# Four places in the output block products of a hybrid encoder layer: a first read, a deviation, a low part and an offset in PSUM

## The chip, the cores and the metric

One core of one Trainium2 chip runs the whole layer in one launch. The metric is the device time of one launch in microseconds (us); the median of several runs is compared. The engines are named as in the profile: PE (TensorE matmuls; PEld its weight loads), DVE (VectorE), ACT (ScalarE), POOL (GpSimd) and SP (SyncE, whose queue issues the DMAs here).

## What is computed

The layer projects 2048 tokens of width 1024, runs a gated linear attention (group A) and a latent softmax attention (group B), gates both, joins them to a 2048 x 1024 matrix and multiplies it by one 1024 x 1024 output matrix. Then comes the residual with a layer norm. The change touches only this last part:

```python
def layer_norm(t, g, b):
    mu = jnp.mean(t32, axis=-1, keepdims=True)
    var = jnp.mean(jnp.square(t32 - mu), axis=-1, keepdims=True)
    y = (t32 - mu) * lax.rsqrt(var + LN_EPS) * g + b
...
    o_b = mla_branch(...)        # ends with  o * jax.nn.silu(gate)
    mixed = jnp.concatenate([o_a, o_b], axis=-1) @ w_out
    x = layer_norm(DEEPNORM_ALPHA * x + mixed, ln_g[layer], ln_b[layer])
```

## The kernel before

The kernel goes through the sequence in 16 chunks of 128 tokens. Every product in fp32 is made of three matmuls: both operands are split into a high part (`hi`, a copy on ACT to the format fp32r, L400) and a low part (`lo`, operand minus high part, here on POOL, L406), and `mm3` (L454 to L456) adds high x high, high x low and low x high in PSUM.

**Chunks 0 to 7** of the output projection are plain: two halves n of 512 columns, eight k-steps each (`OutProj.part`). For each chunk the operand is loaded (`load`), split (`split` calls `op.hi` and `op.lo` for the two halves j = 0, 1; the second half is first multiplied by the gates on POOL, `op.gate`, L2271), multiplied, added to ALPHA * x on DVE (`residual`, L2320) and normalised: `finish_a` on DVE (statistics, then (row - mean) * ln_g, L2336), `rsqrt` on ACT in six small steps (L2342 to L2347), `finish_b` on DVE (row * scale + ln_b, L2353) and the store.

`op.ln` holds the two vectors ln_g and ln_b, first as copies in SBUF (`ln_sb`, the tiles lng and lnb); `ln_psum(0)` and `ln_psum(1)` copy them on ACT (L2220) into two PSUM tiles, and what is traced after that reads them there.

**Chunks 8 to 15** are done in four pairs (class `Pair`, p = 0 to 3). A pair takes two chunks (r = 0 is the odd one, r = 1 the even one) and the two halves of their columns as 2 x 2 blocks A11, A12, A21, A22 and forms the four output blocks with seven products instead of eight (Winograd's form of Strassen's scheme). DVE makes four sums S1 to S4 of the blocks (`add`, L2030): S1 = A21 + A22, S2 = S1 - A11, S3 = A11 - A21, S4 = A12 - S2; each operand is split into high and low part (A11h, A11l and so on). The gates of A12 and A22 are two multiplications on POOL each (`gate`, L2018). The products are P1 (A11), P5 (S1), P6 (S2), P3 (S4), P7 (S3), P2 (A12) and P4 (A22), in this order in pairs 0 to 2; the last pair has P2 ahead of P7, and P4 in two halves. They go to four PSUM banks: P1 and P7 to bank 0, P5 and P2 to bank 1, P6 to bank 2, P3 and P4 to bank 3 (in the last pair P2 to bank 0 and P7 to bank 1).

Each product is read on DVE into the output blocks: `read` (R1 for P1, R5 and R5b for P5, R2, R3, R4b for sums in bank 2, R6 for P3, R7 for P2, R4 for P4). The first read of a block is row = ALPHA * x + bank (L2065), further ones add (L2067). So R1 reads bank 0 and needs the x rows, which `load_res` fetches. `c1` and `c7` (`copy`, L2055, tile pc) copy bank 0 to SBUF on ACT, and `U2`, `U3` (`sum`, L2058) add that copy to bank 2 on DVE.

A finished pair is normalised while the next one runs. Row 1: statistics and `finish_a`, `rsqrt`, `finish_b`, as above. Row 0: `squares` on ACT (sum and sum of squares, L2083 to L2087, called sq in the table of places), `scale` on ACT (called rs: L2092, L2093 and then the six steps of `rsqrt`), `centre` on DVE (L2098), then `finish_b`. In pair 2 the last step is `finish_off` on ACT and POOL instead.

**What sets the order.** Every step of this part is put on one list with a place in us (`put`), counted from the start T of its pair; pairs are 19.05 us apart. The list is sorted, traced in that order, and `in_order` ties each instruction to the one before it on its engine. So a place is not a time: it only says what goes ahead of what on each engine, and an instruction that waits holds all behind it on its engine. Accesses of two engines to one PSUM tile are put in the order in which they are traced, reads too. The places of pairs are in `PLACE_PAIR`: `add`, `hi`, `lo`, `gate` and `gate0` to `gate2` for the loads and splits; `read` for pairs 0 to 2, `read_last` for pair 3; `first` and `second` override some of `add`, `hi` and `lo` for pairs 0 and 1:

```python
second=dict(lS4=-0.85),
first=dict(hA11=-15.2, hS3=-8.0, hA12=0.9, lS3=-6.5, aS4=0.3, hS4=0.35, lS4=0.4),
```

A pair's places below zero stand among those of the pair before: the gates of pair 3 (`gate`, -19.94 to -21.3 and so on) are at -5.67, -2.25, -0.89 and 0.47 of pair 2. Chunks 4 and 5 and the splits of 6 and 7 are written out by hand (`fixed`), with the order kept on ACT, POOL and SP only.

Of the kernel before, what the change touches and what calls it, by code (L numbers as in the profile page):

```python
# [84 lines left out]
    lo=(11.99, 11.22, 11.21, 12.62, 11.98, 11.51, 10.87, 10.63),  # L85
# [23 lines left out]
    lo=(15.35, 16.07, 20.38, 20.41, 24.45, 25.82, 33.5, 36.25),  # L109
# [24 lines left out]
PAIR0, PAIR_US = 8, 19.05  # L134
# [5 lines left out]
    gate=((-19.94, -18.58), (-24.72, -21.3)),  # L140
    add=dict(S1=-10.55, S3=-9.85, S2=-7.6, S4=-0.95),
    hi=dict(A11=-17.26, S1=-9.75, S2=-7.0, A12=-2.0, S3=-4.77, S4=-0.9, A22=-2.66),
    lo=dict(A11=-13.14, S1=-8.45, S2=-6.5, S3=-3.67, A22=1.77, A12=3.13, S4=4.49),
    product=dict(P1=0.0, P5=2.72, P6=5.44, P3=8.16, P7=10.88, P2=13.6, P4=16.32),
    last=dict(P1=0.0, P5=2.72, P6=5.44, P3=8.16, P2=10.88, P7=13.6, P4=16.32),
    gate2=((-11.9, -10.6), (-18.0, -16.7)),
# [1 line left out]
    gate0=((-6.0, -4.7), (-24.72, -21.3)),  # L148
    second=dict(lS4=-0.85),
    first=dict(hA11=-15.2, hS3=-8.0, hA12=0.9, lS3=-6.5, aS4=0.3, hS4=0.35, lS4=0.4),  # L150
    read=dict(c1=2.78, R1=5.9, R5=6.5, R5b=7.1, U2=9.9, R2=10.5, R6=11.3, c7=14.91, U3=15.63, R3=16.26, bn22=16.89,
              R7=17.52, sq=18.25, R4=20.34, R4b=20.97, bn21=21.6, rs=21.9, fa=(22.9, 22.23), fb=(23.9, 26.7), late=(24.2, 24.8)),
    lnb=-1.5,
    read_last=dict(c1=2.78, R1=3.3, R5=6.3, R5b=6.9, U2=8.9, R2=9.5, R3=10.1, R4b=10.7, R6=11.5, bn12=12.1,
                   R7=14.1, bn11=14.7, R3p=16.9, R4p=17.5, bn22=18.1, fa=(15.3, 20.2), fb=(17.0, 20.3)),
)
# [62 lines left out]
    lo=(-0.5, 0.357),  # L219
# [79 lines left out]
    lo=(-0.452, -1.813),  # L299
# [65 lines left out]
    lo=(-0.124, 0.045),  # L365
# [24 lines left out]
class K:  # L390
# [1215 lines left out]
    def attention(self):  # L1606
# [4 lines left out]
        with ExitStack() as ctx:  # L1611
# [214 lines left out]
            op = OutProj(self, ctx, qp, bp, sp, pS, pM, pX, pO, pA)  # L1826
# [5 lines left out]
            def put(place, fn, *a):  # L1832
                todo.append((place, len(todo), fn, a))
# [23 lines left out]
            for k in range(NK):  # L1857
                if k < PRE_W:
                    v = NP * (PRE_BLOCK + k)
                    hi, lo = v + out["pre_hi"], v + out["pre_lo"]  # L1860
                else:
                    hi = end + out["w_hi"] + (k - PRE_W) * out["w_step"]
                    lo = hi + out["w_lo"]
# [30 lines left out]
            late = dict(last)  # L1894
# [8 lines left out]
            def split(c):  # L1903
                if c < NCH:
                    op.hi(rest[c], 0)
                    op.lo(rest[c], 0)
                    op.gate(rest[c])
                    op.hi(rest[c], 1)
                    op.lo(rest[c], 1)

            pairs = [Pair(op, p, PAIR0 + 2 * p + 1, PAIR0 + 2 * p) for p in range((NCH - PAIR0) // 2)]
            with fixed():
                load(4)
                for c in (2, 3):
                    op.load_res(rest[c])
                load(5)
                split(4)
                load(6)
                op.load_res(rest[4])
                for c in (0, 1):  # L1920
                    op.finish(rest[c])
                split(5)
                load(7)
                op.load_res(rest[5])
                op.fetch_t("2l")
                op.fetch_t("3h")
                for c in (2, 3):
                    op.residual(rest[c], 0)
                    op.residual(rest[c], 1)
                    op.finish(rest[c])  # L1930
            for c in (4, 5):
                with fixed():
                    if c == 4:
                        split(6)
                        pairs[0].load(1)
                        op.product(rest[4])
                    else:
                        op.load_res(rest[6])
                        tsum(nb - 1)
                        with self.after(rest[4]["last"]):  # L1940
                            rcp(nb - 1)
                        op.product(rest[5])
                        op.ln_psum(0)
                        pairs[1].load(0, "of")
                        op.fetch_t("3m")
                        split(7)
                        pairs[0].load(0)
                    op.finish(rest[c])
                if c == 4:
                    with self.after(*last.values()), fixed():  # L1950
                        for f in (tot, oh, ol):
                            f(nb - 1)
# [13 lines left out]
                put(t + 2 * half + (5 if c == 6 else 4), op.finish_b, o)  # L1966
            for place, f in ((5.4, turn), (5.41, y), (6.5, rows), (6.51, yc)):
                put(place, f, nb - 1)
            put(3.5, op.ln_psum, 1)
            put(17.15, op.fetch_t, "4h")  # L1970
            put(17.16, op.fetch_t, "4l")
            op.last_pair = pairs[-1]
# [7 lines left out]
class Pair:  # L1980
# [131 lines left out]
    def put(self, put, T, last):  # L2112
# [24 lines left out]
        if last:  # L2137
            reads = (("R1", 0, 0, 0), ("R5", 1, 1, 1), ("R5b", 0, 1, 1), ("R2", 0, 1, 2), ("R3", 1, 1, 2), ("R4b", 1, 0, 2),
                     ("R6", 0, 1, 3), ("R7", 0, 0, b["P2"]), ("R3p", 1, 1, b["P7"]), ("R4p", 1, 0, b["P7"]))
        else:  # L2140
            at(e["c7"], self.copy, bank[b["P7"]])
            at(e["U3"], self.sum, bank[2])
            reads = (("R1", 0, 0, 0), ("R5", 1, 1, 1), ("R5b", 0, 1, 1), ("R2", 0, 1, 2), ("R6", 0, 1, 3), ("R3", 1, 1, 2),
                     ("R7", 0, 0, b["P2"]), ("R4", 1, 0, 3), ("R4b", 1, 0, 2))
        for n, r, h, x in reads:
# [277 lines left out]
```

## Time and profile before

| | us |
|---|---|
| median of 3 runs (lowest, highest) | 1287.73 (1287.08, 1287.99) |
| the profiled execution, its own time | 1284.93 |
| its span, first to last instruction | 1283.2 |
| PE busy | 1255.9 (98%) |
| DVE busy | 940.3 (73%) |
| ACT busy | 875.0 (68%) |
| POOL busy | 851.2 (66%) |

The mean granted clock of PE is 0.998. In a list in order of time a row has the start in us, the busy time in us, the engine, the line, the operation, out<-in with the tiles' names, the shape, the count of instructions that are merged into the row, and in brackets the idle time ahead of it with what ended it. Successive instructions of one engine overlap a little, so a row's start can lie before the end of the row ahead. A row of waits has the total, the number of times and the longest.

In this profile pair 0's P1 starts at 1195.03 us, pair 1's at 1214.07, pair 2's at 1234.53 and pair 3's at 1256.13; the last matmul starts at 1275.21.

### The profile page before, as it was taken

How to read it: one execution, taken by the hardware profiler on the slowest of the kernel's cores; microseconds unless marked ns; L12 is line 12 of the kernel's file. 1: busy time of each engine (PE TensorE's matmuls, PEld its weight loads, DVE VectorE, ACT ScalarE, POOL GpSimd, SP SyncE). 2: the span in 40 equal slices, each digit the busy share in tenths (PEclk: the TensorE clock that was granted, in tenths of full speed). 3: DMA queues.
4: the chain of work that ended last, by engine and by line, in shares of the span. 5: the costliest groups of instructions: out<-in, count | busy, mean ns of one | idle time of the engine just before them, and what ended most of it. 6: DMA issues, size and time to landing. Idle time of an engine off the chain costs nothing.

```text
span 1283.2 us, 20179 instructions
## 1 busy us (share of the span) xinstructions
PE 1255.9 (98%) x6928; PEld 1109.2 (86%) x6928; DVE 940.3 (73%) x1702; ACT 875.0 (68%) x1553; POOL 851.2 (66%) x550
## 2 busy tenths in 40 slices
PE   7999999999999999999999999999999999999997
PEld 7999999999989999999788888888888888788876
DVE  6866674656675445555798888888888888648887
ACT  6765657666675665665688888888888888613455
POOL 0244545363657666672188888889999999955774
PEclk9999999999999999999999999999999999999999
DMA  9332525343575565555501111121223211468952
GB/s 297 94 97 63 168 79 161 99 151 104 185 249 164 178 226 189 181 194 169 172 1 41 42 42 41 42 58 58 58 58 91 58 49 37 169 211 310 333 186 93
DMA packets 122518, 166.81 MB, mean 130 GB/s; under 512 B 18502, under 2 KB 71118, under 8 KB 121776
## 3 DMA queue, kind: packets, MB, share of 16 engines
q1 hardware_dynamic: 114256, 163.39, 40.0%
q0 software_dynamic: 768, 2.10, 0.5%
q8 instruction: 55, 0.90, 0.3%
q10 hardware_dynamic: 7392, 0.03, 0.3%
q14 instruction: 47, 0.39, 0.2%
HBM read 106.72 MB, written 58.75 MB: 129 GB/s over the span
## 4 chain that ended last, share of the span: by engine, by line
PE 56%; POOL 3%; issue 3%; DVE 3%; DMA 3%; ACT 2%; SPq 0%; DVEq 0%; POOLq 0%; ACTq 0%
PE pS L1640 4%; PE pS L1641 4%; PE pS L1642 4%; PE pS L1643 4%; PE pS L1644 4%; PE o L454 4%; PE o L455 4%; PE o L456 4%; PE pz L455 2%; PE pz L456 2%; PE pz L454 2%; PE ipm L456 1%; PE ipm L454 1%; PE ipm L455 1%; POOL of L2271 1%
## 5 line engine op out<-in xcount | busy, mean ns | idle before, releaser
L406 POOL TENSOR_TENSOR pl<-s,ph 128x1024 fp32r<-128x1024 f32 x128 | 306.0, 2414 | 56.6 <-ACT ph L400 56.6
L1662 DVE TENSOR_TENSOR rm<-pS,rm 128x512 f32<-128x512 f32 x210 | 144.9, 690 | 26.3 <-ACT s L1649 20.7
L1686 DVE TENSOR_TENSOR s<-s,mb 128x1024 f32<-128x1024 f32 x128 | 151.3, 1214 | 9.4 <-PE mb L1680 9.3
L1649 ACT ACTIVATE s<-pS 128x1024 f32<-128x1024 f32 x128 | 131.2, 1025 | 37.8 <-PE pS L1644 33.7
L400 ACT ACTIVATE ph<-s 128x1024 fp32r<-128x1024 f32 x128 | 134.9, 1057 | 13.5 <-PE o L456 12.7
L1690 ACT ACTIVATE s<-s 128x1024 f32<-128x1024 f32 x128 | 131.4, 1050 | 13.4 <-DVE s L1686 13.3
L454 PE MATMUL ipa<-wah,xah 128*128 128x384 f32 (+1 forms) x384 | 130.4, 339 | 6.7 <-ACT wah L400 6.7
L1103 POOL TENSOR_TENSOR Us<-Us,cw 128x512 f32<-128x512 f32 x16 | 18.6, 1162 | 174.9 <-DVE Us L1101 159.3
L455 PE MATMUL ipa<-wal,xah 128*128 128x384 f32 (+1 forms) x384 | 125.1, 326 | 0.1
L456 PE MATMUL ipa<-wah,xal 128*128 128x384 f32 (+1 forms) x384 | 125.1, 326 | 0.0
L1640 PE MATMUL pS<-qh,ckvT_h 128*128 128x512 f32 x256 | 102.6, 401 | 0.8 <-DVE rm L1662 0.4
L454 PE MATMUL o<-ph,vh 128*128 128x512 f32 x256 | 101.2, 395 | 0.0
L1641 PE MATMUL pS<-ql,ckvT_h 128*128 128x512 f32 x256 | 100.0, 391 | 0.0
L1642 PE MATMUL pS<-qh,ckvT_l 128*128 128x512 f32 x256 | 100.0, 391 | 0.0
L1643 PE MATMUL pS<-rh,krs 128*128 128x512 f32 x256 | 99.9, 390 | 0.0
L456 PE MATMUL o<-ph,vl 128*128 128x512 f32 x256 | 99.9, 390 | 0.0
L1644 PE MATMUL pS<-rl,krs 128*128 128x512 f32 x256 | 99.9, 390 | 0.0
L455 PE MATMUL o<-pl,vh 128*128 128x512 f32 x256 | 99.8, 390 | 0.0
L1713 DVE TENSOR_TENSOR ap<-ap,s 128x512 f32<-128x512 f32 x120 | 83.1, 693 | 3.6 <-ACT s L1690 0.9
L454 PEld LDWEIGHTS ipa<-wah,xah 128*128 128x128 f32 x384 | 73.2, 191 | 7.7 <-ACT wah L400 7.1
L454 PE MATMUL pz<-xch,wzh 128*128 128x256 f32 x256 | 74.9, 293 | 0.0
L455 PEld LDWEIGHTS ipa<-wal,xah 128*128 128x128 f32 x384 | 73.3, 191 | 1.4 <-DVE wal L406 0.8
(446 smaller groups left out, 3901.7 us busy)
## 6 DMA issues: line engine op xcount, KB each, us to landing
xcf<-xT_dram SPq DMA_DIRECT2D x16, 512.0 KB, 5.6
xr<-x_dram SPq DMA_DIRECT2D x16, 512.0 KB, 6.7
xaf<-xT_dram SPq DMA_DIRECT2D x14, 512.0 KB, 3.8
wb<-wO_dram SPq DMA_DIRECT2D x16, 256.0 KB, 3.1
oib<-oi_s SPq DMA_DIRECT2D x16, 256.0 KB, 4.2
qdb<-qd_s SPq DMA_DIRECT2D x16, 256.0 KB, 4.8
SU<-su_s SPq DMA_DIRECT2D x16, 256.0 KB, 4.8
ub<-u_s SPq DMA_DIRECT2D x16, 256.0 KB, 4.4
```

The source lines that it names most:

```text
L400: return nc.scalar.activation(dst, src, AF.Copy).ins
L406: return e.tensor_tensor(dst, src, hi.bitcast(F32), ALU.subtract).ins
L454: mm(out, ah, bh, start=start, stop=False)
L455: mm(out, ah, bl, start=False, stop=False)
L456: mm(out, al, bh, start=False, stop=stop)
L1640: mm(ps[:, e], kh, qh, start=True, stop=False)
L1641: mm(ps[:, e], kh, ql, start=False, stop=False)
L1642: mm(ps[:, e], kl, qh, start=False, stop=False)
L1643: mm(ps[:, e], kr, rh, start=False, stop=False)
L1644: mm(ps[:, e], kr, rl, start=False, stop=True)
L1662: V.tensor_tensor(d["rm"], src[:, e], d["rm"], ALU.max)
L1686: V.tensor_tensor(s, s, d["mb"][:, None, :].to_broadcast([P, 2, QB]), ALU.subtract)
```

## The change

Four edits, none of which adds or removes an instruction:

1. `read`: R1 of pairs 0 to 2 has the place 2.77 instead of 5.9. It is traced ahead of the copy c1 (2.78) instead of behind it, and on DVE ahead of `finish_a` (T + 3.18), `centre` (T + 3.85) and the first `finish_b` (T + 4.85) of the pair before. In pair 0 it comes between `finish_a` and `finish_b` of chunk 7.
2. `read`: rs, the `scale` of row 0, has 20.8 instead of 21.9, which is 1.75 of the next pair: on ACT ahead of A11h of the pair after that (1.79) and of the next pair's c1 (2.78) instead of behind both.
3. `lo`: S4's low part has -0.895 instead of 4.49. On POOL in pair 2 it goes ahead of both gates of pair 3's row 0 (-0.89, 0.47) and of A22l (1.77) and A12l (3.13); in pair 3 ahead of A22l and A12l. Pairs 0 and 1 keep their overrides.
4. `ln_psum(1)` is called in the split of chunk 7, behind the split of its first half and ahead of its gate, instead of at 3.5 of chunk 6. On ACT the copy goes ahead of the split of chunk 7's second half and of chunk 5's `rsqrt`, and chunk 5's `finish_b` reads ln_b in PSUM instead of SBUF.

```diff
     add=dict(S1=-10.55, S3=-9.85, S2=-7.6, S4=-0.95),
     hi=dict(A11=-17.26, S1=-9.75, S2=-7.0, A12=-2.0, S3=-4.77, S4=-0.9, A22=-2.66),
-    lo=dict(A11=-13.14, S1=-8.45, S2=-6.5, S3=-3.67, A22=1.77, A12=3.13, S4=4.49),
+    lo=dict(A11=-13.14, S1=-8.45, S2=-6.5, S3=-3.67, A22=1.77, A12=3.13, S4=-0.895),
...
-    read=dict(c1=2.78, R1=5.9, R5=6.5, R5b=7.1, U2=9.9, R2=10.5, R6=11.3, c7=14.91, U3=15.63, R3=16.26, bn22=16.89,
-              R7=17.52, sq=18.25, R4=20.34, R4b=20.97, bn21=21.6, rs=21.9, fa=(22.9, 22.23), fb=(23.9, 26.7), late=(24.2, 24.8)),
+    read=dict(c1=2.78, R1=2.77, R5=6.5, R5b=7.1, U2=9.9, R2=10.5, R6=11.3, c7=14.91, U3=15.63, R3=16.26, bn22=16.89,
+              R7=17.52, sq=18.25, R4=20.34, R4b=20.97, bn21=21.6, rs=20.8, fa=(22.9, 22.23), fb=(23.9, 26.7), late=(24.2, 24.8)),
...
             def split(c):
                 if c < NCH:
                     op.hi(rest[c], 0)
                     op.lo(rest[c], 0)
+                    if c == PAIR0 - 1:
+                        op.ln_psum(1)
                     op.gate(rest[c])
...
             for place, f in ((5.4, turn), (5.41, y), (6.5, rows), (6.51, yc)):
                 put(place, f, nb - 1)
-            put(3.5, op.ln_psum, 1)
```

## Prediction, made before the changed kernel was run

> **What bounds the kernel now.** I read the page first, then the waits of TensorE over the last 100 us, then the lists in order of time of DVE (VectorE), ACT (ScalarE) and POOL (GpSimd) for the same stretch. All four edits lie behind 1175 us; the 1175 us before are untouched.
>
> ```profile
> span 1283.2 us, 20179 instructions
> ...
> PE 1255.9 (98%) x6928; PEld 1109.2 (86%) x6928; DVE 940.3 (73%) x1702; ACT 875.0 (68%) x1553; POOL 851.2 (66%) x550
> ```
>
> PE is busy 98% of the span, so only its rare gaps or the tail behind its last product can be won. These are its longest waits from 1180 us on (total, times, longest):
>
> ```profile
> PE pw L456 <- POOL S4l L406: 2.3, 1, 2.3
> PE pw L454 <- DVE xr L2065: 0.6, 1, 0.6
> PE po L454 <- ACT yc L1814: 0.3, 1, 0.3
> ```
>
> Three edits each aim at one: S4's low part at the 2.3, the first read R1 (L2065) at the 0.6, the copy into PSUM at the 0.3. Their sum, 3.2 us (and a little at each restart, whose first matmul takes 0.50 instead of 0.39 us in the rows below), would be the gain if PE set the end. It does so only by little. In the last pair (3), DVE's read R7 waits for P2, and from there DVE works to the end with no wait above 0.41 us:
>
> ```profile
> 1269.93 0.69 DVE L2067 TENSOR_TENSOR xr<-pw,xr 128x512 f32<-128x512 f32 x1 [1.30 <-PE pw L456]
> ...
> 1278.79 1.40 DVE L2353 SCALAR_TENSOR_TENSOR xr<-xr,ln_r,ln 128x512 f32<-128x512 f32 x2 [0.41 <-ACT ln_r L2347]
> ```
>
> So DVE has just 1.30 us of slack there. If PE comes 3 us earlier, what counts is how much earlier DVE comes to R7. DVE runs a loop of its own through the pairs: each pair's products are read and the rows of the pair before are finished before the adds for the next pair come; the S1 adds of pairs 2 and 3 are at 1228.08 and 1248.39 (rows below).
>
> **S4's low part.** Pair 2, in order of time on POOL, and the stall:
>
> ```profile
> 1236.72 1.76 POOL L2018 TENSOR_TENSOR lnb<-lnb,gr 128x512 f32<-128x512 f32 x1
> ...
> 1237.36 0.64 ACT L400 ACTIVATE S4h<-of 128x512 fp32r<-128x512 f32 x1 [2.42 <-DVE of L2030]
> ...
> 1239.15 2.68 POOL L2018 TENSOR_TENSOR lng<-lng,gr 128x512 f32<-128x512 f32 x2 [0.66 <-DMA lng<-ob_s]
> ...
> 1244.24 1.28 POOL L406 TENSOR_TENSOR S4l<-of,S4h 128x512 fp32r<-128x512 f32 x1
> ...
> 1245.58 0.50 PE L456 MATMUL pw<-woh,S4l 128*128 128x512 f32 x1 [2.27 <-POOL S4l L406]
> ```
>
> S4h is ready at 1237.99 (1237.36 + 0.63), but S4l stands behind two gates of pair 3 and two low parts and ends at 1245.52; PE starts 0.06 later. With place -0.895 it goes ahead of both gates (-0.89): it starts when the gate on lnb ends (1238.48) and ends near 1239.8, some 3 us ahead of PE. The stall goes whole. Its price: the two gates start at 1239.8 instead of 1239.15 and take 2.68; A22l, A12l and then A11l of pair 3 follow, three low parts of 1.25 (S4l's row), the last of them ending at 1246.2. P7 and P2, which come next on PE, need S3l, long done, and A12l, there at 1245.0, before P2 at 1247.9 or later; pair 3 needs A11l 10 us on. Pairs 0 and 1 have overrides and keep their order; in pair 3 S4l goes ahead of two low parts and POOL waits for S4h, at nothing, since PE was not waiting there. S4l also takes another buffer of the ring, one whose reader (P4 of the pair before) ends before S4h exists.
>
> **R1 first, and the first row's deviation.** DVE and ACT in pair 2, where the previous pair's rows are finished:
>
> ```profile
> 1237.25 0.39 PE L454 MATMUL pw<-wt1h,S1h 128*128 128x512 f32 x1
> ...
> 1239.41 0.21 DVE L2333 BATCH_NORM_AGGREGATE mv<-bn 128x2 f32<-128x12 f32 x1
> ...
> 1241.04 1.28 DVE L2098 SCALAR_TENSOR_TENSOR xr<-xr,nm,ln 128x1024 f32<-128x1024 f32 x1
> ...
> 1243.96 1.41 DVE L2353 SCALAR_TENSOR_TENSOR xr<-xr,ln_r,ln 128x512 f32<-128x512 f32 x2 [1.64 <-ACT ln_r L2347]
> 1245.28 1.88 DVE L2065 SCALAR_TENSOR_TENSOR xr<-xr,pw 128x512 f32<-128x512 f32 x3
> 1247.07 1.40 DVE L2353 SCALAR_TENSOR_TENSOR xr<-xr,ln_r,ln 128x512 f32<-128x512 f32 x2
> 1248.39 0.69 DVE L2030 TENSOR_TENSOR s<-lnb 128x512 f32<-128x512 f32 x1
> ...
> 1240.72 0.62 ACT L400 ACTIVATE A11h<-lng 128x512 fp32r<-128x512 f32 x1
> 1241.25 0.58 ACT L2055 ACTIVATE pc<-pw 128x512 f32<-128x512 f32 x1
> 1241.72 0.19 ACT L2092 ACTIVATE v<-sq 128x1 f32<-128x1 f32 x1
> ...
> 1243.83 0.19 ACT L2342 ACTIVATE ln_l<-u 128x1 f32<-128x1 f32 x1
> ...
> 1245.17 0.29 ACT L2347 ACTIVATE ln_r<-ln_t,ln_y 128x1 f32<-128x1 f32 x1
> ```
>
> The order on DVE is: S4 add, statistics, finish_a of row 1 (1239.41), centre of row 0 (1241.04), a wait of 1.64 for row 0's scale, finish_b of row 0 (1243.96), R1, R5, R5b (three in 1.88), finish_b of row 1, S1 add. ACT: the squares, over when the split A11h starts (1240.72), A11h, the copy pc, then the deviation (1241.72 to 1243.83, 2.11 us), then row 1's.
> After the change R1 stands ahead of finish_a. It needs P1, done when PE starts P5 (1237.25), and the x rows; both are there at 1239.4. So 0.6 us moves ahead of the centre, which ends at 1242.3 + 0.6 = 1242.9. On ACT the deviation starts at 1240.72 and ends at 1242.83. The two meet: finish_b of row 0 starts at 1242.9 instead of 1243.96, R5 at 1244.2 instead of 1245.9. Row 1's deviation comes behind A11h (0.53) and pc (0.47), at 1243.83, exactly as before, and ends at 1245.46, so its finish_b starts at 1245.5 instead of 1247.07. **DVE gains 1.57 us per pair**, in pairs 1 and 2. The copy pc ends 2.1 us later, 1243.8; P7, which writes its bank, comes at 1244.9 at the earliest: covered by 1 us. R1 no longer holds P7.
>
> **What takes part of it back: adds against POOL.** The S adds read two operands from SBUF, and where such an instruction meets one of POOL, one of them stretches:
>
> ```profile
> 1182.40 2.44 DVE L2353 SCALAR_TENSOR_TENSOR rr<-rr,ln_r,lnb 128x512 f32<-128x512 f32 x2 [2.00 <-ACT ln_r L2347]
> ...
> 1182.94 3.06 POOL L2018 TENSOR_TENSOR of<-of,gr 128x512 f32<-128x512 f32 x2 [0.75 <-DMA of<-ob_s]
> ...
> 1204.98 1.29 POOL L406 TENSOR_TENSOR A12l<-of,A12h 128x512 fp32r<-128x512 f32 x1
> 1206.24 1.28 POOL L406 TENSOR_TENSOR A11l<-lng,A11h 128x512 fp32r<-128x512 f32 x1
> ...
> 1206.36 1.72 DVE L2030 TENSOR_TENSOR s<-lnb 128x512 f32<-128x512 f32 x1
> ```
>
> The S1 add of pair 1 (1206.36) took 1.72 instead of 0.69: it ran once A11l had ended (1207.52). At 1182.40 two such instructions of DVE (0.75 each when alone, half of row 1247.07 being 0.70) took 2.44: POOL's gate came during the first, got its turn between them, and held the second 1 us. I take this turn-taking for the rule here. Pair 1: R1 now fills the wait for finish_b of chunk 7, so S1 comes 0.6 earlier, 1205.76, inside A12l (to 1206.27); it runs to 1206.9, A11l then runs to 1208.1, S3 behind it to 1208.8. Before, S3 followed S1's end (1208.08) and ended at 1208.8 too. Gain: none. Pair 2:
>
> ```profile
> 1225.18 2.70 POOL L2018 TENSOR_TENSOR of<-of,gr 128x512 f32<-128x512 f32 x2
> ...
> 1228.08 0.69 DVE L2030 TENSOR_TENSOR s<-of 128x512 f32<-128x512 f32 x1
> 1228.80 0.69 DVE L2030 TENSOR_TENSOR of<-of,of 128x512 f32<-128x512 f32 x1
> ```
>
> 1.57 earlier, S1 comes at 1226.5, between the two gates (1225.18 and about 1226.5, end 1227.88), which POOL does in one burst set off by S4h of pair 1, not earlier than before. Whoever goes first, two adds of 0.65 and a gate of 1.3 follow from 1226.5: S3 ends at 1229.1 instead of 1229.49. Gain kept: 0.4. Pair 3: S1 comes at 1248.39 - 0.4 - 1.57 = 1246.4; POOL's A11l ends at 1246.2 - 0.4 = 1245.8, so nothing meets. S4's add of pair 3 meets nothing either, as POOL then waits for S4h. So DVE enters the last pair **1.95 us earlier** (0.4 + 1.57).
>
> The Trainium skill (SBUF — State Buffer, Who interferes with whom) says that a VectorE instruction with two SBUF inputs and a GpSimd instruction that reads SBUF exclude each other, the one issued first holding for its whole length; the 1.72 agrees. [...]
>
> **The last pair.** Here the order turns against the change:
>
> ```profile
> 1256.89 0.74 DVE L2030 TENSOR_TENSOR lng<-lng 128x512 f32<-128x512 f32 x1
> ...
> 1261.04 0.58 ACT L2055 ACTIVATE pc<-pw 128x512 f32<-128x512 f32 x1
> ...
> 1261.65 0.69 DVE L2065 SCALAR_TENSOR_TENSOR xr<-xr,pw 128x512 f32<-128x512 f32 x1 [0.22 <-ACT pc L2055]
> ```
>
> The last pair's own R1 keeps its place behind the copy, and it waited for that copy (0.22). The deviation of pair 2 now comes ahead of the copy: R1 starts 2.11 us later, counted from the S4 add of 1256.89. DVE's idle 1.30 before R7 is used up by that: 2.11 - 1.30 = 0.81 lost. P2, for which R7 waited until 1269.9, ends about 3 us earlier (2.4 of the stall and its restart, 0.5 of the waits before it), 1267.0, and R7 comes at 1268.8: PE is not waited for.
> Sum: -1.95 + 0.81 = **-1.14 us** at R7, and so at the end.
>
> **The offset in PSUM.** The 1.01 us copy moves into ACT's wait for a gate:
>
> ```profile
> 1180.19 0.63 ACT L400 ACTIVATE oh<-of 128x512 fp32r<-128x512 f32 x1 [4.02 <-POOL of L2271]
> ...
> 1182.27 1.01 ACT L2220 ACTIVATE ln<-lnb 128x1024 f32<-128x1024 f32 x1
> ```
>
> It needs the banks that DVE's reads of chunk 5 empty; if they were read only 3 us into that wait it would still fit into the 4.02. yc comes 1 us earlier and PE's 0.3 goes (up to 0.6 with the restart); chunk 5's finish_b ends up to 1 us earlier. Both end in slack: DVE, which sets the end, waits for gates and scales later on. Value at the end: 0; bounds -0.6 and 0.
>
> **Against the measured time.** The profiled execution took 1284.93 us, 1.7 above its span and 2.8 below the median of 1287.73. A difference carries over: profiled 1283.8, median **1286.6**. Bounds of this case: gain at S3 of pairs 1 and 2 between 0 and 0.9, so -0.7 to -2.0.
>
> **Rivals.** (1) *The adds slip through*: the second add follows the first ahead of POOL, or POOL's spans, which are rough, leave room. The adds then lose what they lost before and no more: 0.6 in pair 1, 1.57 in pairs 2 and 3, 3.74 in all; end -3.74 + 0.81 = -2.9, at most -3.7 if the 1.03 held at 1206.36 goes too: 1284.8. [...] For it: 1.7 us of the working hang on two collisions that the trace of before does not have, at places where tenths decide, and the adds at 1248.39 and 1228.80 show 0.69, unheld. Against: the 2.44.
> (2) *R1 waits for its x rows*: R1 was 6 us later and could not be held by the load; now it heads the DVE queue, with finish_a, centre, finish_b and the adds behind it.
>
> ```profile
> 1232.24 1.09 SPq L2014 DMA_DIRECT2D xr<-x_dram  x2
> DMA to landing us min/median/max: 2.0/4.0/7.5
> ```
>
> At the slowest landing recorded, 7.5, the first is there at 1239.7, a hold of 0.7 against R1 at 1239.0. The end is 1.14 - hold earlier, so slower from a landing after 1240.2; a landing at 1243.5 (11 us) gives a hold of 4.5, +3.4: 1291.1. Against: the load is issued a microsecond earlier too, as the stores ahead of it are.
> (3) *The reordering changes nothing at the end* (within 0.3): the last pair's 2.11 eats all; X would have to be 0.8 instead of 1.95.
>
> **How the numbers follow.** Forecast 0.46, rival 1 0.40, rival 2 0.07, rival 3 0.07. About 0.2%, 2.6 us, is what a measurement of this kernel can tell from no change. Faster by more: rival 1 and a little of the forecast's tail, 0.42. Slower by more: most of rival 2, 0.05. The rest, 0.53, lies within. The range runs from rival 1 (with some of its extra), 1284.2, to no change, 1287.8; the forecast's own is 1285.7 to 1287.0.
>
> **What would show it.** S4l of pair 2 right behind the gate on lnb and no PE wait on POOL; R1 of pairs 0 to 2 right behind the statistics, finish_b of row 0 with a wait under 0.2; S3 of pairs 1 and 2 at 1.7 instead of 0.69 (0.69 would mean rival 1); R1 of the last pair waiting about 2.3 for the copy, and R7 not waiting for PE. R1 waiting for a DMA would be rival 2. If the last R1 does not wait for the copy, or the end follows PE, the sum is wrong.

## The result, and the profile after

| | before | after |
|---|---|---|
| median, us (lowest to highest, 15 runs each) | 1285.98 (1282.71 to 1288.63) | 1282.91 (1280.59 to 1284.11) |
| ratio, 95% interval | | 0.9977 (0.9967 to 0.9987) |
| the profiled execution, its own time, us | 1284.93 | 1283.54 |
| its span, us | 1283.2 | 1281.7 |

The change makes the kernel faster, by 0.23% or 3.0 us (1.7 to 4.2). A gain of 1.14 us was forecast. The kernel before came out 1.75 us lower than the median that the prediction started from; the 15 runs contain those three, and the other 12 have a median of 1284.87.

To read the traces alike, three marks on DVE are used from here on: the start of the last attention reduction (L1770), which lies ahead of everything that the change touches; the start of pair 0's S4 add; and the start of the last `finish_b`. The first stretch is called the lead-in, the second the pairs. In the execution of the kernel before that the prediction read they are 28.63 and 80.14 us, by these starts and the 1278.79 already shown (list in order of time, before):

```profile
1170.02 0.67 DVE L1770 TENSOR_REDUCE rc<-sx 128x4 f32<-128x512 f32 x1
...
1185.42 0.69 DVE L2320 SCALAR_TENSOR_TENSOR rr<-xr,pmb 128x512 f32<-128x512 f32 x1 [0.58 <-issue]
...
1198.65 1.77 DVE L2030 TENSOR_TENSOR of<-of 128x512 f32<-128x512 f32 x1 [1.74 <-POOL of L2018]
...
1216.27 0.68 DVE L2030 TENSOR_TENSOR lng<-lng 128x512 f32<-128x512 f32 x1
...
1236.59 0.74 DVE L2030 TENSOR_TENSOR of<-of 128x512 f32<-128x512 f32 x1
```

After the change, PE's waits from 1185 us on hold nothing of POOL and nothing of R1; one row is left (total, times, longest), with the busy times from the page:

```profile
PE pw L454 <- DVE xr L2068: 0.8, 2, 0.7
```

```profile
span 1281.7 us, 20184 instructions
...
PE 1255.0 (98%) x6928; PEld 1108.3 (86%) x6928; DVE 941.1 (73%) x1702; ACT 876.2 (68%) x1553; POOL 852.7 (67%) x550
```

The lines of the pairs stand one further down than before. Pair 2 after the change, in order of time, DVE, ACT, POOL and PE:

```profile
1237.17 1.28 POOL L406 TENSOR_TENSOR S4l<-of,S4h 128x512 fp32r<-128x512 f32 x1
1238.42 2.66 POOL L2019 TENSOR_TENSOR lng<-lng,gr 128x512 f32<-128x512 f32 x2
...
1238.80 0.69 DVE L2066 SCALAR_TENSOR_TENSOR xr<-xr,pw 128x512 f32<-128x512 f32 x1 [0.69 <-PE pw L456]
...
1239.58 0.20 ACT L2093 ACTIVATE v<-sq 128x1 f32<-128x1 f32 x1
...
1241.02 1.28 DVE L2099 SCALAR_TENSOR_TENSOR xr<-xr,nm,ln 128x1024 f32<-128x1024 f32 x1
...
1241.70 0.62 ACT L400 ACTIVATE A11h<-lng 128x512 fp32r<-128x512 f32 x1
...
1242.40 1.41 DVE L2354 SCALAR_TENSOR_TENSOR xr<-xr,ln_r,ln 128x512 f32<-128x512 f32 x2
...
1243.85 0.39 PE L456 MATMUL pw<-woh,S4l 128*128 128x512 f32 x1
...
1246.24 0.68 DVE L2031 TENSOR_TENSOR s<-lnb 128x512 f32<-128x512 f32 x1
```

S4l goes ahead of both gates of lng and PE takes it without a wait: the 2.27 us stall is gone. R1 stands behind the statistics, the deviation ahead of A11h, and `finish_b` of row 0 follows the centre without a wait (1.64 before). But R1 waits 0.69 us at the head of DVE's queue. The row puts that down to PE; P1 had been done 2.9 us earlier (PE began P5 at 1235.91), and a second execution of the same kernel names the true releaser (below).

### The profile page after: what moved, and what is told of

Its sections match the earlier page's. It is cut to its first block, busy times and chain, and to the rows that moved or that the text cites. A ratio compares the mean times of both kernels' runs of the same rounds, so it can differ in the third digit from the quotient of the medians.

```text
span 1281.7 us, 20184 instructions
## 1 busy us (share of the span) xinstructions
PE 1255.0 (98%) x6928; PEld 1108.3 (86%) x6928; DVE 941.1 (73%) x1702; ACT 876.2 (68%) x1553; POOL 852.7 (67%) x550
## 4 chain that ended last, share of the span: by engine, by line
PE 75%; DVE 6%; ACT 5%; POOL 4%; DMA 3%; issue 3%; SPq 0%; DVEq 0%; POOLq 0%; ACTq 0%
PE pS L1640 4%; PE pS L1641 4%; PE pS L1642 4%; PE pS L1643 4%; PE pS L1644 4%; PE o L454 4%; PE o L455 4%; PE o L456 4%; PE ipa L454 3%; PE ipa L456 3%; PE ipa L455 3%; PE pz L455 2%; PE pz L456 2%; PE pz L454 2%; PE ipg L454 2%
## 5 line engine op out<-in xcount | busy, mean ns | idle before, releaser
L1662 DVE TENSOR_TENSOR rm<-pS,rm 128x512 f32<-128x512 f32 x210 | 144.8, 690 | 26.4 <-ACT s L1649 20.8
L1690 ACT ACTIVATE s<-s 128x1024 f32<-128x1024 f32 x128 | 131.5, 1050 | 13.4 <-DVE s L1686 13.3
```

What stands on the lines that cost most here:

```text
L1662: V.tensor_tensor(d["rm"], src[:, e], d["rm"], ALU.max)
```

## Experiments

The table has every profiled execution: the two stretches, how long R1 of pair 2 waited, and the ratio to the kernel before of the timed runs (a dash: one profiled execution, no timed runs). In the expectations, theory A is the prediction's working (the end follows DVE), rival B that all of PE's waits are gained, rival C that the pairs differ from execution to execution; D to G are explained where they come up.

| kernel | lead-in | pairs | sum | R1's wait | ratio (95%) |
|---|---|---|---|---|---|
| before | 28.63 | 80.14 | 108.77 | | |
| before, three more | 28.43, 28.98, 29.00 | 80.23, 79.84, 79.65 | 108.66, 108.82, 108.65 | | 1.0001 (0.9991 to 1.0011), -, - |
| after | 28.23 | 79.17 | 107.40 | 0.69 | 0.9977 (0.9967 to 0.9987) |
| after, three more | 28.23, 27.79, 27.51 | 79.35, 78.87, 78.67 | 107.58, 106.66, 106.18 | 0.88, 0.39, 0.20 | 0.9982 (0.9972 to 0.9992), -, - |
| S4l alone | 28.93 | 78.83 | 107.76 | | 0.9991 (0.9982 to 1.0000) |
| offset alone | 28.12 | 79.44 | 107.56 | | 0.9989 (0.9978 to 1.0001) |
| after, offset undone | 28.53 | 80.34 | 108.87 | 1.87 | 0.9993 (0.9985 to 1.0002) |
| after, S4l undone | 27.72 | 80.67 | 108.39 | 0.78 | 0.9983 (0.9973 to 0.9993) |
| after, rs undone | 27.73 | 78.29 | 106.02 | 0.75 | 0.9975 (0.9965 to 0.9985) |
| after, last R1 first | 27.99, 27.37 | 76.66, 78.33 | 104.65, 105.70 | 0, 1.94 | 0.9968 (0.9957 to 0.9980), 0.9967 (0.9955 to 0.9979) |
| after, x rows early | 27.94 | 78.62 | 106.56 | 0 | 0.9977 (0.9966 to 0.9989) |
| after, both of these | 28.50 | 76.67 | 105.17 | 0 | 0.9964 (0.9951 to 0.9977) |

**The kernel before against itself.** No edit.

> The kernel before, unchanged, timed against itself. Theory A (the change is worth 1.1 to 1.5 us, as in its trace; the rest of the 3 us between the medians is the spread of executions): ratio within 0.9985 to 1.0015, executions several us apart, and the trace of this execution shows the same waits of PE in the pairs (2.3 for S4l, 0.6 for R1) and R7 of the last pair waiting 1.3 for PE, while any difference in the span lies ahead of the pairs. Rival B (the whole 3.2 us that PE waited has been gained): the same ratio, but no drift ahead of the pairs. Rival C (the pairs of the kernel before differ from execution to execution, and the change takes the bad cases away): the waits of PE in this trace differ from those of the first one by a microsecond or more.

Measured: 1.0001 with an interval of a tenth of a percent to either side, and a trace whose two stretches repeat within 0.2 us. PE's waits are as theory A expected (2.0 for S4l, 0.7 for R1). Two later executions of the same kernel spread each stretch by 0.6 us, the long lead-ins with the short pairs, but the sum by 0.17 only: where one trace is compared with another, the sum is the better measure. One thing is alike in all four: R7 of the last pair waits for PE, 1.30 us in the first, 1.16 in this one (the row) and 1.09 and 0.92 in the later two:

```profile
1270.55 0.69 DVE L2067 TENSOR_TENSOR xr<-pw,xr 128x512 f32<-128x512 f32 x1 [1.16 <-PE pw L456]
```

So in the kernel before the end follows PE, and DVE has about 1 us to spare there.

**S4's low part alone**, on the kernel before:

```diff
-    lo=dict(A11=-13.14, S1=-8.45, S2=-6.5, S3=-3.67, A22=1.77, A12=3.13, S4=4.49),
+    lo=dict(A11=-13.14, S1=-8.45, S2=-6.5, S3=-3.67, A22=1.77, A12=3.13, S4=-0.895),
```

> The kernel before with S4's low part alone moved (-0.895). Theory A: PE's wait of 2.3 us is gone, but DVE comes to R7 of the last pair no earlier than before, so only its 1.3 us of slack are won: -1.1 us (ratio 0.9991), R7 with no wait for PE. Rival B: -2.3 to -2.6 us (ratio 0.998).

Measured: the pairs are 1.14 us shorter than the mean of the four of before (79.97), the sum 0.97 (107.76 against 108.73), timed 1.2 us (0 to 2.3). The stall was 1.8 to 2.3; what arrives at the end is about the 0.92 to 1.30 that DVE had as slack ahead of R7, which now waits 0.14 at most:

```profile
1269.16 0.69 DVE L2067 TENSOR_TENSOR xr<-pw,xr 128x512 f32<-128x512 f32 x1
```

The rest of the stall is lost because from there on DVE sets the end: theory A, not B.

**The deviation back behind A11h and the copy**, on the changed kernel:

```diff
-    ... bn21=21.6, rs=20.8, fa=(22.9, 22.23), ...
+    ... bn21=21.6, rs=21.9, fa=(22.9, 22.23), ...
```

> The changed kernel with the first row's deviation back behind the split and the copy (21.9). Theory A: DVE gains only some 0.4 and 0.7 us per pair through R1, but the last pair's R1 no longer waits 2.1 us for the copy behind the deviation, so this is faster than the whole change: -2.2 us against before (ratio 0.9983), 1.1 us better than the changed kernel. Rival B: no difference to the changed kernel, or a little slower.

Measured: 0.9975, the pairs 78.29. In order of time, DVE:

```profile
1197.84 1.76 DVE L2031 TENSOR_TENSOR of<-of 128x512 f32<-128x512 f32 x1 [1.73 <-POOL of L2019]
...
1223.42 1.40 DVE L2354 SCALAR_TENSOR_TENSOR xr<-xr,ln_r,ln 128x512 f32<-128x512 f32 x2 [1.86 <-ACT ln_r L2348]
...
1227.26 0.68 DVE L2031 TENSOR_TENSOR s<-of 128x512 f32<-128x512 f32 x1
1227.98 0.69 DVE L2031 TENSOR_TENSOR of<-of,of 128x512 f32<-128x512 f32 x1
...
1247.03 0.68 DVE L2031 TENSOR_TENSOR s<-lnb 128x512 f32<-128x512 f32 x1
...
1260.29 0.69 DVE L2066 SCALAR_TENSOR_TENSOR xr<-xr,pw 128x512 f32<-128x512 f32 x1 [0.21 <-ACT pc L2056]
...
1276.13 1.41 DVE L2354 SCALAR_TENSOR_TENSOR xr<-xr,ln_r,ln 128x512 f32<-128x512 f32 x2 [0.41 <-ACT ln_r L2348]
```

The wait for row 0's scale is back (1.86 in pair 1), but S3 of pair 2 no longer meets POOL (0.69), and the last pair's R1 waits 0.21 for its copy instead of 2.46. From pair 0's S4 add to pair 3's S1 add it is 1.14 us longer than the changed kernel (49.19 against 48.05), from there to the end 2.02 shorter (29.10 against 31.12). In these two traces, with nearly the same hold of pair 2's R1 (0.75 and 0.69), this edit on top of the other three costs 0.88 us, where theory A expected 1.1; the timed ratio cannot tell.

**The last pair's R1 ahead of its copy too**, on the changed kernel, run twice:

```diff
-    read_last=dict(c1=2.78, R1=3.3, R5=6.3, ...
+    read_last=dict(c1=2.78, R1=2.77, R5=6.3, ...
```

> The changed kernel with the last pair's R1 too ahead of its copy (place 2.77 instead of 3.3 in the places of the last pair). Theory A: the wait of 2.5 us for the copy on DVE goes; R7 then waits for PE again (P2 of the last pair ends 3.4 us earlier than in the kernel before), so the end is 2 to 2.4 us earlier than in the changed kernel's trace: -3.0 to -3.7 us against before (ratio 0.997). Rival B: no difference to the changed kernel.

> The version with the last pair's R1 ahead of its copy, once more, beside the two runs with the x rows earlier. Both theories: ratio 0.9968 again. What it tells: whether the hold of pair 2's R1 was absent before by luck of that execution (theory E: 0 to 1.9 us of hold this time, and the stretch from the last attention reduction to the last finish_b longer than 104.65 by just that).

Measured: 0.9968 and 0.9967. First execution, DVE in order of time:

```profile
1257.64 0.67 DVE L2066 SCALAR_TENSOR_TENSOR xr<-xr,pw 128x512 f32<-128x512 f32 x1
...
1266.79 0.69 DVE L2068 TENSOR_TENSOR xr<-pw,xr 128x512 f32<-128x512 f32 x1 [0.62 <-PE pw L456]
...
1275.58 0.75 DVE L2354 SCALAR_TENSOR_TENSOR xr<-xr,ln_r,ln 128x512 f32<-128x512 f32 x1 [0.41 <-ACT ln_r L2348]
```

The wait of 2.46 is gone and R7 waits for PE again, 0.62. Against the changed kernel without a hold (78.62, further below) the pairs lose 1.96 more, 76.66. In the traces this version is shorter than both kernels. Its timed ratios lie below the changed kernel's 0.9977 and 0.9982, but their intervals overlap. In its second execution R1 of pair 2 was held 1.94 us and the pairs are longer by 1.67: the hold varies from execution to execution and goes nearly whole into the pairs. The sum was expected to grow by just the hold; it grew by 1.05, as the lead-in of that execution was 0.62 shorter.

**The changed kernel again, and the offset.** Three kernels with the kernel before in turn: the change as it is; with the offset's copy back in its old place; and with that edit alone, on the kernel before.

> The changed kernel once more, timed against before. Theory A (in its first trace the pairs, from the S4 add of pair 0 to the last finish_b, took 1.0 us less than before, and what lies ahead of them 0.5 less): -1.5 us (ratio 0.9988), the pairs again at 79.2 us, the last R1 waiting 2.4 to 2.5 us for the copy and R7 not waiting for PE. Rival B (the first timing, 0.9977, is the true size, -3 us): ratio 0.9977 again, and pairs a microsecond or more shorter than 79.2.

> The changed kernel with the copy of the offset back in its old place, so that chunk 5 reads it in SBUF. Theory A as it stood in the prediction: no difference to the changed kernel. Theory D (the second instruction of chunk 5's finish_b is held by a gate on POOL, and behind it on DVE stand chunk 6's residual and pair 0's first add): 0.5 to 0.7 us slower than the changed kernel, 28.4 to 28.9 us instead of 27.7 to 28.2 from the reduction of the last attention block to pair 0's S4 add, and chunk 5's finish_b at 2.4 us or more instead of 1.41.

> The kernel before with the copy of the offset alone moved. Prediction: 0 (its cover was said to be DVE's later waits). Theory D: -0.5 to -0.7 us (ratio 0.9995), all of it ahead of pair 0's S4 add (28 us from the last reduction instead of 28.4 to 28.9), and the pairs as before, 80.1 to 80.2 us, with PE's wait of 2 us or more for S4l. Rival B: PE's 0.3 alone, -0.3.

Measured: the changed kernel's second set gives 0.9982, whose interval holds theory A's 0.9988 and rival B's 0.9977 alike; its trace is as A said (pairs 79.35, the last R1 waiting 2.46 for its copy, R7 not waiting for PE).

The lead-in is 27.37 to 28.50 us in the eleven executions with the offset read from PSUM, mean 27.92, and 28.43 to 29.00 in the six without, mean 28.75. **The offset's edit takes 0.83 us off the lead-in**, which is theory D with a little more than its 0.5 to 0.7. With it undone, chunk 5's `finish_b` (DVE and POOL, in order of time):

```profile
1180.83 2.99 POOL L2018 TENSOR_TENSOR of<-of,gr 128x512 f32<-128x512 f32 x2
...
1181.08 3.29 DVE L2353 SCALAR_TENSOR_TENSOR rr<-rr,ln_r,lnb 128x512 f32<-128x512 f32 x2 [2.01 <-ACT ln_r L2347]
1184.29 0.68 DVE L2320 SCALAR_TENSOR_TENSOR rr<-xr,pmb 128x512 f32<-128x512 f32 x1
...
1238.98 0.69 DVE L2065 SCALAR_TENSOR_TENSOR xr<-xr,pw 128x512 f32<-128x512 f32 x1 [1.87 <-DMA xr<-x_dram]
```

and in the changed kernel:

```profile
1169.96 0.67 DVE L1770 TENSOR_REDUCE rc<-sx 128x4 f32<-128x512 f32 x1
...
1177.45 1.03 ACT L2221 ACTIVATE ln<-lnb 128x1024 f32<-128x1024 f32 x1 [1.32 <-DVE rr L2321]
...
1182.11 2.66 POOL L2019 TENSOR_TENSOR of<-of,gr 128x512 f32<-128x512 f32 x2
...
1182.37 1.41 DVE L2354 SCALAR_TENSOR_TENSOR rr<-rr,ln_r,ln 128x512 f32<-128x512 f32 x2 [2.01 <-ACT ln_r L2348]
1184.92 0.69 DVE L2321 SCALAR_TENSOR_TENSOR rr<-xr,pmb 128x512 f32<-128x512 f32 x1 [1.15 <-issue]
...
1198.19 1.76 DVE L2031 TENSOR_TENSOR of<-of 128x512 f32<-128x512 f32 x1 [1.81 <-POOL of L2019]
```

With its offset in SBUF the two instructions take 2.44 to 3.29 us while POOL's gates run, and chunk 6's residual stands right behind them. With the offset in PSUM they take 1.41 in the midst of the same gates. Not all of the 1.0 to 1.9 arrives, since the residual waits for a second thing too (1.15 in the row above), most likely its x rows, whose load goes out some 8.5 us after the reduction; no trace records their landing. Counted from the reduction, the residual starts at 15.21 to 15.61 in the six executions with the offset in SBUF (mean 15.51): in four of them as soon as `finish_b` ends, in two after a wait of 0.38 or 0.58 for the second thing. With the offset in PSUM it starts at 14.10 to 15.24 (mean 14.64), each time after a wait. From there to the S4 add it is 12.9 to 13.4 us in all seventeen executions: what the residual gains carries through pair 0's first adds and its gates.

How much of this reaches the end is less certain, with one trace for each. In the changed kernel with the offset undone the sum is 108.87, 0.6 above what the changed kernel would have at that hold of 1.87 (worked out below). With the offset's edit alone it is 107.56, 1.17 below the mean of before: more than theory D's 0.5 to 0.7, and not with the pairs unchanged as D said, for they are 79.44. PE no longer waits for the output block's copy yc (0 to 0.7 in the four traces of before) nor for R1 of pair 1 (0.6 to 0.7), and R7 still waits for PE, 0.73, so the end follows PE there. Timed, neither stands clear of noise: 0.9989 (0.9978 to 1.0001), and 0.9993 against the changed kernel's 0.9982.

The second execution of the changed kernel shows R1's releaser (DVE and SP's queue, in order of time):

```profile
1228.55 1.08 SPq L2015 DMA_DIRECT2D xr<-x_dram  x2
...
1236.95 0.69 DVE L2066 SCALAR_TENSOR_TENSOR xr<-xr,pw 128x512 f32<-128x512 f32 x1 [0.88 <-DMA xr<-x_dram]
```

**S4's low part undone**, on the changed kernel (place 4.49 again):

> The changed kernel with S4's low part back behind the gates. Theory A: PE stands 2 to 3.5 us for S4l in pair 2, and R7 of the last pair waits for PE again, since DVE comes early enough: the pairs take 0.3 us more than the changed kernel's 79.2, no more, as DVE's late last R1 hides the rest; against before -1.1 us with what is won ahead of the pairs (ratio 0.999). Rival B (PE sets the end): 2.3 us slower than the changed kernel.

Measured: 0.9983, but the profiled execution, the slowest of its eleven runs, shows pairs of 80.67. PE waits, and DVE in order of time:

```profile
PE pw L456 <- POOL S4l L406: 1.8, 1, 1.8
```

```profile
1269.95 0.69 DVE L2068 TENSOR_TENSOR xr<-pw,xr 128x512 f32<-128x512 f32 x1 [1.27 <-PE pw L456]
```

R7 waits 1.27 us for PE: without S4's edit what DVE gains ends there. In the trace the edit is worth about 1.4 us in the pairs (80.67 against 79.2, the 78.62 and the hold of 0.78 less 0.2). Theory A expected 0.3 and rival B 2.3: by this trace it is neither. The timed ratio cannot tell the two kernels apart.

**The x rows ahead of the next pair's loads**, on the changed kernel, and on the version with the last R1 first:

```diff
-    res=(-10.0, -8.0),
+    res=(-12.46, -8.0),
```

> The changed kernel with one edit more: in every pair the x rows of the first row are asked for ahead of the next pair's loads instead of behind them. In the profiled executions so far R1 of pair 2, which now heads DVE's queue, was held by these rows 0.69, 0.88 (the changed kernel), 0.75, 1.87 and 0.78 us (its variants). Theory E (the second rival of the prediction, in small: the hold sets what DVE gains): the hold of R1 in pairs 1 and 2 is gone, from the last attention reduction to the last finish_b 106.6 us instead of 107.4 and 107.6, and the ratio lies 0.0006 below the changed kernel's. Rival (the hold is hidden, DVE only waits elsewhere, for the first row's scale or the gates): the hold goes, the total stays within 0.3 us, ratio as the changed kernel's 0.998. Rival (the delayed loads of the next pair hold the gates): slower by up to 0.5 us.

> The same edit on the version in which the last pair's R1 is read ahead of its copy too. Its profiled execution had no hold of R1 by x rows and came out at 104.65 us from the last attention reduction to the last finish_b, so theory E expects the same there in a profile (104.5 to 104.8) and a ratio 0 to 0.0006 below that version's 0.9968; the rival that the hold is hidden expects 0.9968.

Measured on the changed kernel, in order of time:

```profile
1226.90 0.44 SPq L2015 DMA_DIRECT2D xr<-x_dram  x1
...
1241.18 0.67 DVE L2066 SCALAR_TENSOR_TENSOR xr<-xr,pw 128x512 f32<-128x512 f32 x1
...
1244.99 1.41 DVE L2354 SCALAR_TENSOR_TENSOR xr<-xr,ln_r,ln 128x512 f32<-128x512 f32 x2 [0.33 <-ACT ln_r L2348]
```

The load goes out 14.3 us ahead of R1, instead of 8.4 in the second execution of the changed kernel, and R1 waits for nothing. The pairs are 78.62, and the four executions of the changed kernel follow from it as 78.62 plus the hold less 0.2 (79.17, 79.35, 78.87 and 78.67 with holds of 0.69, 0.88, 0.39 and 0.20); the 0.2 is part of the 0.33 that `finish_b` would wait for its scale anyway. So the traces bear theory E out, 106.56 where it gave 106.6; the ratio, 0.9977, shows nothing of the 0.06% that it expected, which is too small for its interval. On the other version the pairs, 76.67, repeat its unheld 76.66, but the sum of 105.17 misses the 104.5 to 104.8 that was expected, since the lead-in was 28.50. The ratio of 0.9964 is the lowest measured, but not apart from 0.9967.

**Four more profiled executions**, two of each kernel, on one chip:

> The kernel before, one more profiled execution. From the start of the last attention reduction to the start of the last finish_b it took 108.8 and 108.7 us in two executions. Theory F (this stretch is fixed in the kernel before): 108.5 to 108.9 again. Rival G (it varies, and two traces of it came out short): up to 110.

> The changed kernel, one more profiled execution; 107.4 and 107.6 us so far over the same stretch, with R1 of pair 2 held 0.69 and 0.88 us by its x rows. Theory F: 106.6 plus the hold (0, 0.8 or 1.9 us have been seen), less 0.2, so 106.6 to 108.3. Rival G: the mean of the four traces of the changed kernel lies 2 us or more under that of the four of the kernel before.

> As the first of these looks at the kernel before: 108.5 to 108.9 by theory F, up to 110 by rival G.

> As the first of these looks at the changed kernel: 106.6 plus the hold of R1 less 0.2 by theory F.

Measured: theory F for the kernel before, whose four sums lie within 108.65 and 108.82. The changed kernel's lie between 106.18 and 107.58. The two taken here come out at 106.66 and 106.18 where the hold alone gave 106.8 and 106.6, the second below theory F's bound; the rest is a shorter lead-in. Means: 108.73 and 106.96, so the traces show **1.77 us**: 0.82 in the lead-in, 0.95 in the pairs. Rival G expected 2 or more. Counted instead from the start of PE's last matmul for that reduction (L1763), the means are 117.89 and 116.15, so the gain does not hang on the mark.

## Why the prediction was wrong

**What held.** The mechanism of the pairs came as worked out. By the starts of S4 adds and S1 adds in the two profiles: from pair 2's S4 add to pair 3's S1 add 11.80 us became 10.93, which is the 1.57 forecast less the hold of 0.69. From pair 1's S4 add to pair 2's S4 add 0.45 of 1.57 was kept, forecast 0.4. From pair 3's S1 add to the end it got 0.72 longer, forecast 0.81. The turn-taking with POOL, which decided between the forecast and rival 1, is there in both pairs:

```profile
1205.29 1.08 DVE L2031 TENSOR_TENSOR s<-lnb 128x512 f32<-128x512 f32 x1
...
1205.78 1.74 POOL L406 TENSOR_TENSOR A11l<-lng,A11h 128x512 fp32r<-128x512 f32 x1
...
1206.40 1.67 DVE L2031 TENSOR_TENSOR lnb<-lng,lnb 128x512 f32<-128x512 f32 x1
...
1215.44 0.68 DVE L2031 TENSOR_TENSOR lng<-lng 128x512 f32<-128x512 f32 x1
...
1224.41 3.20 POOL L2019 TENSOR_TENSOR of<-of,gr 128x512 f32<-128x512 f32 x2
...
1225.77 0.68 DVE L2031 TENSOR_TENSOR s<-of 128x512 f32<-128x512 f32 x1
1226.49 1.66 DVE L2031 TENSOR_TENSOR of<-of,of 128x512 f32<-128x512 f32 x1
...
1235.31 0.74 DVE L2031 TENSOR_TENSOR of<-of 128x512 f32<-128x512 f32 x1
```

S3 takes 1.67 and 1.66 instead of 0.69, as foretold. Rival 1's -2.9 us, which equals the timed gain, is thus no explanation of it. POOL had its turn between two adds that follow each other at once.

The last pair, where R1 is held by its copy and R7 no longer waits for PE:

```profile
1261.13 0.58 ACT L2056 ACTIVATE pc<-pw 128x512 f32<-128x512 f32 x1
...
1261.74 0.69 DVE L2066 SCALAR_TENSOR_TENSOR xr<-xr,pw 128x512 f32<-128x512 f32 x1 [2.46 <-ACT pc L2056]
...
1268.59 0.67 DVE L2068 TENSOR_TENSOR xr<-pw,xr 128x512 f32<-128x512 f32 x1
...
1277.36 1.41 DVE L2354 SCALAR_TENSOR_TENSOR xr<-xr,ln_r,ln 128x512 f32<-128x512 f32 x2 [0.41 <-ACT ln_r L2348]
```

**The step that failed: "The offset in PSUM ... Both end in slack ... Value at the end: 0; bounds -0.6 and 0."** The lead-in, where the sum had nothing, is 0.83 us shorter with it, beyond the bound; by the two traces, 0.6 or 1.17 of it reach the end. The prediction had the row that says so, 2.44 us for two instructions of 0.75, and even used it for the turn-taking; but it took the slack behind them from DVE's waits much later, for gates and scales, without asking whether those gates and scales hang on the same chain. They do: the residual of chunk 6 and pair 0's first adds stand on DVE behind that `finish_b`, and the splits and gates of pair 0 follow from them. In the trace that it read there was slack right behind `finish_b`, the residual's wait of 0.58; in four of the six executions with the offset in SBUF there was none. The sizes of the pairs' terms, by contrast, add up to 0.95 in the traces, not far from 1.14.

**The second rival came true in small.** Its hold was worked out as 0.7 at the slowest landing recorded, and it was given a chance of 0.07. The row of landings beside it, with a median of 4.0, mixes the loads of x rows with the stores of finished rows, which use the same tiles. The loads alone (L2014) in the same trace:

```profile
DMA to landing us min/median/max: 4.0/6.7/7.5
```

A landing of 6.7 would already be within 0.1 us of R1's new start, and for the load in question itself the trace records none: that its rows are there by 1239.4 was assumed. Measured were 0 to 1.94 us in nine executions with R1 first and the load in its place; eight of them had a hold. In the execution with SP's row, R1 starts 8.4 us after the load is issued. This takes off up to 1.7 of the pairs' gain; without it the pairs would have given 1.35 (79.97 less 78.62), near the 1.14 of the sum. That nearness is partly luck: in pair 1 0.37 was gained where the sum had nothing, mostly because S3 ended earlier.

**The range.** It ended at 1284.2, and the measured median is 1282.9. Of the 3.7 us between forecast and median, 1.75 are the starting value: the kernel before measured 1285.98 there, and its medians in three more sets of 27, 33 and 15 runs were 1285.01, 1284.89 and 1285.46, so the three runs within 0.9 us of each other, from which the median of 1287.73 came, were no bound for where the next set would lie. The profiled execution of 1284.93, which the prediction noted as 2.8 below that median and then set aside, was nearer to it. Moved down by 1.75, the range would begin at 1282.5 and hold the measured median, so the step headed "Against the measured time", which takes the gain off the median of those three runs, failed too. The other 1.9 are the change, of which the offset is 0.8 and the rest not accounted for. One sum of rival 1 is off as well: with the 1.03 it would be -3.96 by its own terms, not -3.7.

**What stays open.** Timed gains of 3.0 and 2.3 us stand against 1.77 in the traces. Both intervals (1.7 to 4.2 and 1.0 to 3.6) include it, so there may be nothing to explain. The spans of the eight profiled executions differ by 3.1 us in the mean, and 1.3 of that lies ahead of the last attention reduction, where nothing was changed. Its start lies between 1167.9 and 1173.4 us over all executions; a share of the gain that lay there could not be told from that scatter. No run has R1's new place alone or undoes it alone, so what it gives by itself was not measured.

## What to carry to other kernels

An operand that is moved from SBUF to PSUM can shorten a whole chain, when a VectorE instruction with two SBUF operands stands among GpSimd's and ahead of that chain on its queue (here 0.83 us): price it by what stands behind it, not by a later wait of the engine, and look at several executions before calling a wait slack. When a read is moved to the head of an engine's queue, move its load too, and take the load's landing from a row of that load alone. When small steps are pulled ahead of a copy, look for the one place (here the last pair) where somebody waits for that copy. Make the sum on a stretch between two marks around the change, in several executions, and let the range for a median take in how the kernel before scatters from set to set.

## What was not expected of the hardware

The same scaled add of 128x512 took 1.41 us for two with its second operand in PSUM in the midst of POOL's gates, and 2.44 to 3.29 us with it in SBUF. In one execution the x rows were there only 8.4 us after issue, with the next pair's eight loads issued in the 6.8 us ahead of them, and the wait for them ranged from 0 to 1.94 us over nine executions; issued ahead of those loads, in two executions, they were not waited for.
